# A streaming encoder layer: gate and history loads on GpSimd's queue, gated stores on ScalarE's, new pooling state copied from scratch

## The chip, the cores and the metric

The kernel runs on one core of a Trainium2 chip. The core has a matmul engine (TensorE, PE; its weight loads are listed as PEld), a vector engine (VectorE, DVE), a scalar engine (ScalarE, ACT), GpSimd (POOL) and SyncE (SP, used here to issue DMAs). Each engine works through its own instructions in order; DMAs issued by an engine go through that engine's queue to the shared DMA engines. The metric is the device time of one launch in microseconds (us).

## The reference

One layer for a prompt of 1024 tokens and 8 streams of 16 new tokens each. Cut to what matters here:

```python
xn = rms_norm(x, norm_g)
u, g_pool, c_q, c_kv, k_r, g_mla = jnp.split(xn @ w_in, SPLIT_IDX, axis=-1)
# for each of 4 groups of 256 channels, window w in (2, 4, 8, 16):
#   d = trailing mean over w tokens of u (with 15 tokens of history) - u
#   out = d @ w_pool[group]
pool_out = out * pool_scale * jax.nn.silu(g_pool)
new_pool = jnp.concatenate([pool_hist, u], axis=1)[:, -POOL_HIST:]     # POOL_HIST = 15
...                                                                    # latent attention -> attn
mla_out = attn * jax.nn.silu(g_mla)
h = x + jnp.concatenate([pool_out, mla_out], axis=-1) @ w_out
y = h + sigmoid(rms_norm(h, ple_norm_g) @ w_ple_gate + b_ple_gate) * (p @ w_ple)
```

For the prompt the history is zero; for each of the 8 streams it is the 15 last rows of its state. `new_pool`, one of the outputs, holds the last 15 rows of u: one set for the prompt and eight for the streams, and it is called `npool` in the kernel.

## The kernel before, in words

All activations lie with channels on the 128 partitions and tokens along the free axis. The 1152 tokens (1024 of the prompt, 128 of the streams) are three blocks t = 0, 1, 2 of 384; the third has the prompt's last 256 tokens and the 128 of the streams. Products are taken in three matmuls of a high and a low part (`wh`, `wl`, written by ScalarE and VectorE from the raw weights `wraw`), L77 to L79 or L175 to L177.

The first phase is the input projection. Its output columns are tiles of 128 channels, taken two at a time ("pairs" m), in the order: latents, then for each of the four groups g two tiles gp (the pool branch's gate) and two tiles u (the pool branch's input), then eight tiles gm (the attention's gate). It runs in two chunks of the reduction: the first leaves partial sums in DRAM scratch, the second reads them back (tile `q`, L512, on SyncE's queue), adds, and calls `finish` on each result `o`, which multiplies, takes Silu of gp and gm on ScalarE (L534), and stores to scratch in DRAM (L535, on GpSimd's queue). In the trace, the source or destination `gp`, `gm`, `u` is that scratch; in the order, `gp0`, `gp1`, `gp2` and `u0`, `u1`, `u2` are the scratch of the three token blocks.

While the second chunk goes on to the next pairs, the mixer works on the group that is done. `mixer(m, i)` is called between the parts of a pair and takes two steps from a list for each call. The steps of a group:
- `fetch` loads a block of u back from scratch on SyncE's queue (tile `u`, two buffers): L704 the 384 tokens, L703 the 15 tokens ahead of them; for t = 2 also L707, the streams' history, from the input `state_pool` into tile `us`.
- `weights` loads `w_pool` (L673, SyncE) and splits it into `pwh`, `pwl`.
- `gates` loads two tiles of Silu(gp) (L713, SyncE) into tile `ev`, which has two buffers.
- `tile` forms the windowed means on VectorE (L689, L693, and L727, L728 for the first tokens), giving `d`. For t = 2 it copies the streams' tokens to `us` and stores the new state from the SBUF tiles to the output, on GpSimd's queue: L730 from `u` (128 x 15), L734 from `us` (128 x 8 x 15, runs of 60 bytes).
- `split` makes `dh` (ScalarE, L68) and `dl` (VectorE, L69).
- `mix` multiplies by the group's weights (TensorE, L77 to L79 into `aux`), scales by pool_scale and the gate on VectorE (L751, into the gate's tile `ev`) and stores to scratch `mixp` on GpSimd's queue (L752).

The program is traced through a tile framework: buffers of a name are reused in turn, an instruction waits by semaphore for those that it depends on, and a scheduler sets the order of each engine's instructions by its own costs. So the place of an instruction in its queue isn't the one in the code. `k.later` and `step` only decide in which order things are traced. After the first phase come the latents and keys, the attention, and the output projection with the embedding gate.

Of the kernel before, what the change touches and what calls it, by code (L numbers as in the profile page):

```python
# [16 lines left out]
NB = 8  # L17
NS = 16
NTOK = SEQ + NB * NS
P = 128  # L20
# [3 lines left out]
HIST = 15  # L24
# [106 lines left out]
class Quick:  # L131
# [47 lines left out]
    def pair(self, c0, c1, A, X, W, prior, done, between):  # L179
# [23 lines left out]
        q = prior and prior(c0, 0)  # L203
        self.product(a, x("11"), W[1], True)
        s1 = tile("s1", 2)
        nc.scalar.activation(s1[:], a, AF.Copy)
        d = bank(c1, 1)
# [45 lines left out]
def phase1(k, sc):  # L253
# [4 lines left out]
    tc, nc, io = k.tc, k.nc, k.io  # L258
# [6 lines left out]
    pp = es.enter_context(tc.tile_pool(name="p1m", bufs=1, space=PSUM, reuse_waits="tile"))  # L265
# [12 lines left out]
    src = [io["w_in"][first[n] + i] for n, i in kinds]  # L278
# [10 lines left out]
    def o_tile():  # L289
        return k.t(xp, [P, TB], "o", bufs=3)  # L290
# [48 lines left out]
    def step(n=1):  # L339
        for _ in range(n):  # L340
            if steps:
                steps.pop(0)()


    raw = k.t(wp, [P, 8, P], "wraw", bufs=3)
# [156 lines left out]
    for n in OPS:  # L502
        for j in range(4):
            raw = k.t(ap, [P, TB], f"a{j}")
# [12 lines left out]
    def latent_factor(kind, t, a):  # L517
        yield
        yield from factors(lp, a, 3, KVR if kind == "ckv" else QR, 3)
        nc.sync.dma_start(sc["s_" + kind][t][:], a[:])  # L520

    def finish(i, t, ps, q):
        kind, n = kinds[i] if i < KR else ("kr", 0)
        o = o_tile()
        if q is not None:
            nc.vector.tensor_tensor(o[:], ps, q[:], ALU.add)
            ps = o[:]
        if t == 2:
            nc.vector.tensor_tensor(o[:], ps, R2[:], ALU.mult)
        if kind == "kr":  # L530
            k.later(rope_key(k, lp, aux_bank, o, kc, ks, t, sc))
            return
        if kind in ("gp", "gm"):
            nc.scalar.activation(o[:], o[:], AF.Silu)  # L534
        nc.gpsimd.dma_start(sc[kind][t][:, n, :], o[:])  # L535
        if kind not in ("ckv", "cq"):
            return
        if (kind, t) not in acc:
            acc[kind, t] = [k.t(lp, [P, TB], f"acc{t}"), 2 if kind == "ckv" else 4]
            nc.scalar.activation(acc[kind, t][0][:], o[:], AF.Square)  # L540
        else:
            sq = k.t(lp, [P, TB], "sq")
            nc.scalar.activation(sq[:], o[:], AF.Square)
            nc.vector.tensor_tensor(acc[kind, t][0][:], acc[kind, t][0][:], sq[:], ALU.add)
        acc[kind, t][1] -= 1
        if not acc[kind, t][1]:
            k.later(latent_factor(kind, t, acc[kind, t][0]))
# [8 lines left out]
    def mixer(m, i):  # L556
        k.tick()
        if m < 5:
            return
        if not mix:  # L560
            assert not k.queue
            ls.close()
            mp = es.enter_context(tc.tile_pool(name="p1p", bufs=1, side="right", reuse_waits="tile"))
            inv = k.t(mp, [P, 16], "inv")
            nc.sync.dma_start(inv[:], io["inv_cnt"])
            mix.append(Pool(k, mp, aux_bank, inv, sc, wp))
        pool = mix[0]
        if m in (5, 7, 9, 11) and i == 0:
            g = (m - 5) // 2
            for t in range(NT):  # L570
                if t == 0:
                    pool.fetch(2 * g, 0)
                steps.append(lambda t=t: (pool.fetch(2 * g + 1, t), pool.tile(2 * g, t)))
                steps.append(lambda t=t: pool.tile(2 * g + 1, t))
                if t:
                    steps.append(lambda t=t: pool.mix(g, t - 1))
                else:
                    steps.append(lambda: pool.weights(g))
                steps.append(lambda t=t: (pool.gates(g, t), t < NT - 1 and pool.fetch(2 * g, t + 1), pool.split()))
            steps.append(lambda: pool.mix(g, NT - 1))  # L580
        step(2)

    chunk(1, prior, finish, mixer, range(KR // 2 - 1), KR - 2 * 3)
    last = KR // 2 - 1
    W = qk.sums(src[2 * last:], 1, True)
    qk.pair(2 * last, 2 * last + 1, A, None, W, prior, finish, lambda i: mixer(last, i))
    qk.tail()
    wn = (qk.hl(qk.raw(src[KR - 2 * 3], 1)), 0)
# [38 lines left out]
def rope_key(k, lp, aux_bank, x, kc, ks, t, sc):  # L627

    nc = k.nc
    yield  # L630
    a = aux_bank()
    av = a[:, :TB].rearrange("p (j c) -> p j c", j=3)
    for j in range(3):
        nc.tensor.transpose(av[:, j, :], x[:, j * P:(j + 1) * P], k.ident[:])
    hl = k.t(lp, [P, 3, P], "krhl")
    nc.scalar.activation(hl[:], av, AF.Copy)
    kr = k.t(lp, [P, 3, DR], "kr")
    nc.vector.tensor_tensor(kr[:], hl[:, :, :DR], hl[:, :, DR:], ALU.add)
    tmp = k.t(lp, [P, 3, DR], "krt")
    nc.vector.tensor_tensor(tmp[:], kr[:], kr[:], ALU.mult)  # L640
    v = k.t(lp, [P, 3], "krv")
    r = k.t(lp, [P, 3], "krr")
    nc.vector.tensor_reduce(v[:], tmp[:], AX.X, ALU.add)
    nc.vector.tensor_scalar(v[:], v[:], 1.0 / DR, EPS, ALU.mult, ALU.add)
    k.rsqrt(lp, r[:], v[:], "krs")
    nc.vector.tensor_tensor(kr[:], kr[:], r[:].unsqueeze(2).to_broadcast([P, 3, DR]), ALU.mult)
    o = k.t(lp, [P, 3, 2, DR], "kro")
    sl = slice(3 * t, 3 * t + 3)
    rotate(k, o[:, :, 0, :], kr[:], tmp[:], kc[:, sl, :], ks[:, sl, :], nc.vector)
    nc.vector.tensor_copy(o[:, :, 1, :], o[:, :, 0, :])  # L650
    nc.sync.dma_start(k.io["krope"][:, sl, :], o[:, :, 0, :])
    yield
    yield
    b = aux_bank()
    for j in range(3):
        nc.tensor.transpose(b[:, j * P:(j + 1) * P], o[:, j, :, :].rearrange("p a c -> p (a c)"), k.ident[:])
    e = k.t(lp, [P, TB], "ev")
    nc.scalar.activation(e[:], b[:, :TB], AF.Copy)
    nc.sync.dma_start(sc["krT2"][t][:], e[:])


class Pool:


    def __init__(self, k, pp, aux_bank, inv, sc, wp):
        self.k, self.pp, self.aux, self.inv, self.sc = k, pp, aux_bank, inv, sc
        self.wp, self.hl, self.d = wp, [None, None], [None, None]
        self.u, self.gate, self.us = {}, {}, {}

    def weights(self, g):  # L670
        k, pp = self.k, self.pp
        raw = k.t(self.wp, [P, 8, P], "wraw", bufs=3)[:, :4, :].rearrange("p (a b) c -> p a (b c)", a=2)
        k.nc.sync.dma_start(raw, k.io["w_pool"][g])  # L673
        self.wh = k.t(pp, [P, 2, 256], "pwh", F32R)
        self.wl = k.t(pp, [P, 2, 256], "pwl", F32R)
        k.split(self.wh[:], self.wl[:], raw)
# [19 lines left out]
    def fetch(self, ct, t):  # L696

        k, nc, src = self.k, self.k.nc, self.sc["u"]
        u = self.u[ct, t] = k.t(self.pp, [P, HIST + TB], "u", bufs=2)
        if t == 0:  # L700
            nc.vector.memset(u[:, :HIST], 0.0)
        else:
            nc.sync.dma_start(u[:, :HIST], src[t - 1][:, ct, TB - HIST:])  # L703
        nc.sync.dma_start(u[:, HIST:], src[t][:, ct, :])  # L704
        if t == NT - 1:
            us = self.us[ct] = k.t(self.pp, [P, NB, HIST + NS], "us", bufs=2)
            nc.sync.dma_start(us[:, :, :HIST], self.k.io["state_pool"][ct])  # L707

    def gates(self, g, t):
        k = self.k  # L710
        for n in (2 * g, 2 * g + 1):
            self.gate[n, t] = k.t(self.pp, [P, TB], "ev", bufs=2)
            k.nc.sync.dma_start(self.gate[n, t][:], self.sc["gp"][t][:, n, :])  # L713

    def tile(self, ct, t):
        k, pp, nc, io = self.k, self.pp, self.k.nc, self.k.io
        g, c2 = divmod(ct, 2)
        w = 2 << g
        d = self.d[c2] = k.t(pp, [P, TB], f"d{c2}")
        n = TB if t < NT - 1 else SEQ - TB * (NT - 1)  # L720
        u = self.u.pop((ct, t))
        s = self.window(u[:, :HIST + n], n, d[:, :n], w)
        if t == 0:

            m = w - 1
            x = k.t(pp, [P, 16], "head")
            nc.vector.tensor_tensor(x[:, :m], s[:, HIST:HIST + m], self.inv[:, :m], ALU.mult)  # L727
            nc.vector.tensor_tensor(d[:, :m], x[:, :m], u[:, HIST:HIST + m], ALU.subtract)  # L728
        if t == NT - 1:
            nc.gpsimd.dma_start(io["npool"][ct][:, 0, :], u[:, n:n + HIST])  # L730
            us = self.us.pop(ct)
            nc.vector.tensor_copy(us[:, :, HIST:], u[:, HIST + n:].rearrange("p (b s) -> p b s", b=NB))
            self.window(us[:], NS, d[:, n:].rearrange("p (b s) -> p b s", b=NB), w, (NB,))
            nc.gpsimd.dma_start(io["npool"][ct][:, 1:, :], us[:, :, NS:])  # L734

    def split(self):
        for c, d in enumerate(self.d):
# [944 lines left out]
```

## Time and profile before

| | |
|---|---|
| runs (us) | 2287.53, 2289.75, 2299.92; median 2289.75 |
| the profiled execution | 2292.38 us, its span 2290.6 us |
| TensorE | 2211.1 us busy, 97% of the span |
| VectorE, ScalarE, GpSimd | 1439.5, 1004.0, 410.8 us busy |
| DMA | 339.24 MB, mean 148 GB/s |

A row of the trace's timeline gives start, duration, engine (SPq is SyncE's issuing of DMAs), line, operation, out<-in, shapes and, in brackets, the idle time ahead of the instruction on its engine with what ended it. The line numbers are those of the kernel before. DMA rows give the time from issue to landing. Where a stretch is given as A:B, it is in us from the span's start. The mixer of the four groups lies between about 515 and 800 us.

### The profile page before, as it was taken

To read this page: it belongs to the slowest core of one execution; us is meant where nothing else is said; L and a number is where in the kernel's file an instruction comes from. 1 tells how busy PE (TensorE), PEld (TensorE's weight loads), DVE (VectorE), ACT (ScalarE), POOL (GpSimd) and SP (SyncE) were. 2 spreads that over 40 slices of the span, in tenths; PEclk is the share of its full clock that TensorE was granted. 3 is DMA by queue.
4 is the path that set the end of the run, shared out by engine and by line. 5 is a ranking of instruction groups with operands and counts; after the bars stand their busy time and mean duration, and the time that the engine had idled before them with its cause. 6 is when DMAs were issued, how large, how long until landed. Compare 5 with 4: busy or idle time off the path is not lost.

```text
span 2290.6 us, 36006 instructions
## 1 busy us (share of the span) xinstructions
PE 2211.1 (97%) x12856; PEld 2154.0 (94%) x12856; DVE 1439.5 (63%) x3008; ACT 1004.0 (44%) x2229; POOL 410.8 (18%) x431
## 2 busy tenths in 40 slices
PE   8989999999898989989999899999999999999999
PEld 7989999999898989989998799999999999999998
DVE  6787776686777667768888765555553345344343
ACT  6533335443333467766666644343342233232232
POOL 0000000111222101034453532221002221111110
PEclk9999999999999999999999899999999999999999
DMA  9565336557766666473221754443263333222221
GB/s 303 178 225 169 125 125 213 166 161 192 190 185 179 216 206 179 130 240 99 93 84 53 241 179 152 128 154 122 85 198 112 101 121 110 86 94 96 85 87 64
DMA packets 241012, 339.24 MB, mean 148 GB/s; under 512 B 37729, under 2 KB 185313, under 8 KB 240833
## 3 DMA queue, kind: packets, MB, share of 16 engines
q1 hardware_dynamic: 217568, 290.77, 41.3%
q0 software_dynamic: 10880, 32.41, 4.4%
q10 hardware_dynamic: 12384, 13.77, 1.9%
q8 instruction: 101, 1.65, 0.3%
q14 instruction: 79, 0.64, 0.1%
HBM read 235.74 MB, written 101.12 MB: 147 GB/s over the span
## 4 chain that ended last, share of the span: by engine, by line
PE 66%; DMA 12%; DVE 9%; issue 8%; ACT 3%; POOL 2%; SPq 0%; ACTq 0%; DVEq 0%; POOLq 0%
PE mm L78 8%; PE mm L77 8%; PE mm L79 8%; PE mm L175 5%; PE mm L176 5%; PE mm L177 5%; PE f L77 3%; PE f L79 3%; PE f L78 3%; PE k L79 2%; PE k L78 2%; PE k L77 2%; DMA u<-u 1%; PE t L1215 1%; PE pb L77 1%
## 5 line engine op out<-in xcount | busy, mean ns | idle before, releaser
L68 ACT ACTIVATE wh<-wraw 128x1024 fp32r<-128x1024 f32 (+3 forms) x207 | 150.2, 729 | 146.3 <-PE mm L177 83.8
L69 DVE TENSOR_TENSOR wl<-wraw,wh 128x512 fp32r<-128x512 f32 (+3 forms) x205 | 172.0, 842 | 66.7 <-ACT wh L68 58.8
L1538 DVE TENSOR_TENSOR ev<-mm,R 128x384 f32<-128x384 f32 x48 | 26.7, 557 | 173.9 <-PE mm L79 170.0
L1539 ACT ACTIVATE ev<-ev,gains 128x384 f32<-128x384 f32 x48 | 29.4, 612 | 224.2 <-DVE ev L1538 124.4
L71 ACT ACTIVATE wh<-wraw,gains 128x128 fp32r<-128x128 f32 x256 | 82.1, 391 | 53.0 <-ACT wh L71 31.9
L72 DVE SCALAR_TENSOR_TENSOR wl<-wraw,gains,wh 128x128 fp32r<-128x128 f32 x256 | 88.0, 390 | 18.0 <-ACT wh L71 16.9
L77 PE MATMUL k<-wkh,ch 128*128 128x448 f32 x256 | 96.1, 376 | 3.2 <-ACT ch L68 2.7
L1216 ACT ACTIVATE pth<-t 128x512 fp32r<-128x512 f32 (+2 forms) x96 | 45.5, 485 | 119.7 <-PE t L1215 117.9
L68 ACT ACTIVATE wh<-wt 128x1024 fp32r<-128x1024 f32 x60 | 63.4, 1056 | 74.0 <-PE mm L177 48.5
L78 PE MATMUL k<-wkh,cl 128*128 128x448 f32 x256 | 94.5, 369 | 0.1
L79 PE MATMUL k<-wkl,ch 128*128 128x448 f32 x256 | 94.6, 369 | 0.0
L69 DVE TENSOR_TENSOR wl<-wt,wh 128x1024 fp32r<-128x1024 f32 x60 | 73.3, 1221 | 24.8 <-ACT wh L68 24.6
L79 PE MATMUL mm<-A2l,wh 128*128 128x384 f32 x256 | 86.0, 336 | 0.0
L77 PE MATMUL mm<-A2h,wh 128*128 128x384 f32 x256 | 86.0, 336 | 0.0
L78 PE MATMUL mm<-A2h,wl 128*128 128x384 f32 x256 | 86.0, 336 | 0.0
L77 PE MATMUL mm<-A0h,wh 128*128 128x384 f32 x256 | 85.8, 335 | 0.0
L79 PE MATMUL mm<-A0l,wh 128*128 128x384 f32 x256 | 85.7, 335 | 0.0
L78 PE MATMUL mm<-A1h,wl 128*128 128x384 f32 x256 | 85.7, 335 | 0.0
L78 PE MATMUL mm<-A0h,wl 128*128 128x384 f32 x256 | 85.7, 335 | 0.0
L77 PE MATMUL mm<-A1h,wh 128*128 128x384 f32 x256 | 85.5, 334 | 0.0
L79 PE MATMUL mm<-A1l,wh 128*128 128x384 f32 x256 | 85.5, 334 | 0.0
L1510 POOL TENSOR_TENSOR R<-R,sq 128x384 f32<-128x384 f32 x45 | 46.0, 1023 | 210.3 <-ACT sq L1509 210.3
(809 smaller groups left out, 7867.2 us busy)
## 6 DMA issues: line engine op xcount, KB each, us to landing
wraw<-w_in SPq DMA_DIRECT2D x89, 512.0 KB, 4.4
part<-o SPq DMA_DIRECT2D x93, 192.0 KB, 2.5
q<-part SPq DMA_DIRECT2D x93, 192.0 KB, 3.1
wraw<-w_out SPq DMA_DIRECT2D x64, 256.0 KB, 3.3
wraw<-w_ple_gate SPq DMA_DIRECT2D x64, 256.0 KB, 3.2
ple<-ev POOLq DMA_DIRECT2D x48, 192.0 KB, 2.9
fev<-xT SPq DMA_DIRECT2D x48, 192.0 KB, 2.5
hp<-fev SPq DMA_DIRECT2D x48, 192.0 KB, 2.1
```

The lines of the kernel that those rows point to most:

```text
L68: nc.scalar.activation(hi, src, AF.Copy)
L69: eng.tensor_tensor(lo, src, hi, ALU.subtract)
L71: nc.scalar.activation(hi, src, AF.Copy, scale=scale)
L72: eng.scalar_tensor_tensor(lo, src, scale, hi, ALU.mult, ALU.subtract)
L77: mm(out, sh, mh, start=start, stop=False)
L78: mm(out, sl, mh, start=False, stop=False)
L79: self.last = mm(out, sh, ml, start=False, stop=stop)
L175: mm(ps, sh, xh[:], start=start and j == 0, stop=False, **kw)
L176: mm(ps, sl, xh[:], start=False, stop=False, **kw)
L177: self.k.last = mm(ps, sh, xl[:], start=False, stop=j == n - 1, **kw)
L1216: nc.scalar.activation(pth[:, :n, qq], tp[:, :n, :], AF.Copy)
L1510: nc.gpsimd.tensor_tensor(acc[t][:], acc[t][:], sq[:], ALU.add)
```

## The change

Three things are moved, and one is done in another way:
- The stores of gp and gm (48) are issued by ScalarE instead of GpSimd. The stores of u and of the latents stay on GpSimd.
- The loads of the gates (24) and of the streams' history (8) are issued by GpSimd instead of SyncE.
- The new pooling state is no longer stored from the SBUF tiles but copied from the scratch of u (block 2) to the output, DRAM to DRAM, in the same two pieces for each channel tile (16 DMAs), on GpSimd's queue as before.
- The load of w_pool is traced earlier in a group: behind the first fetch.

```diff
@@ finish
+        store = nc.gpsimd
         if kind in ("gp", "gm"):
             nc.scalar.activation(o[:], o[:], AF.Silu)
-        nc.gpsimd.dma_start(sc[kind][t][:, n, :], o[:])
+            store = nc.scalar
+        store.dma_start(sc[kind][t][:, n, :], o[:])
@@ mixer
                 if t == 0:
                     pool.fetch(2 * g, 0)
+                    pool.raw_weights(g)
@@ Pool
+    def raw_weights(self, g):
+        self.raw = self.k.t(self.wp, [P, 8, P], "wraw", bufs=3)[:, :4, :].rearrange("p (a b) c -> p a (b c)", a=2)
+        self.k.nc.sync.dma_start(self.raw, self.k.io["w_pool"][g])
+
     def weights(self, g):
-        k, pp = self.k, self.pp
-        raw = k.t(self.wp, [P, 8, P], "wraw", bufs=3)[:, :4, :].rearrange("p (a b) c -> p a (b c)", a=2)
-        k.nc.sync.dma_start(raw, k.io["w_pool"][g])
+        k, pp, raw = self.k, self.pp, self.raw
@@ fetch
-            nc.sync.dma_start(us[:, :, :HIST], self.k.io["state_pool"][ct])
+            nc.gpsimd.dma_start(us[:, :, :HIST], self.k.io["state_pool"][ct])
@@ gates
-            k.nc.sync.dma_start(self.gate[n, t][:], self.sc["gp"][t][:, n, :])
+            k.nc.gpsimd.dma_start(self.gate[n, t][:], self.sc["gp"][t][:, n, :])
@@ tile
         if t == NT - 1:
-            nc.gpsimd.dma_start(io["npool"][ct][:, 0, :], u[:, n:n + HIST])
             us = self.us.pop(ct)
             ...
-            nc.gpsimd.dma_start(io["npool"][ct][:, 1:, :], us[:, :, NS:])
+            src = self.sc["u"][t][:, ct, :]
+            nc.gpsimd.dma_start(io["npool"][ct][:, 0, :], src[:, n - HIST:n])
+            nc.gpsimd.dma_start(io["npool"][ct][:, 1:, :], src[:, n:].rearrange("p (b s) -> p b s", b=NB)[:, :, NS - HIST:])
```

In the changed kernel the stores of `finish` are L537, the histories L708 (u) and L712 (us), the block fetch L709, w_pool L675, the gates L718, the new state L740 and L741, `mixp` L759.

The scheduler's order around the start of the second group, on GpSimd. Names carry a buffer number; `o` is a finished result, `ev` a gate tile. Before:

```order
L752 DMA mixp2_15_74<-ev_1150_5802 128x384
L752 DMA mixp2_15_74<-ev_1151_5804 128x384
L535 DMA u2_27_86<-o_1162_5877 128x384
L535 DMA u2_27_86<-o_1163_5904 128x384
L535 DMA u1_26_85<-o_1184_5986 128x384
L535 DMA u0_25_84<-o_1185_6001 128x384
L535 DMA gp0_7_66<-o_1198_6044 128x384
```

The same place now:

```order
L759 DMA mixp2_15_74<-ev_1150_5802 128x384
L759 DMA mixp2_15_74<-ev_1151_5804 128x384
L537 DMA u2_27_86<-o_1162_5877 128x384
L718 DMA ev_1202_6066<-gp0_7_66 128x384
L718 DMA ev_1203_6068<-gp0_7_66 128x384
L740 DMA npool<-u2_27_86 128x15
L741 DMA npool<-u2_27_86 128x8x15
L537 DMA u2_27_86<-o_1163_5904 128x384
L740 DMA npool<-u2_27_86 128x15
L741 DMA npool<-u2_27_86 128x8x15
L537 DMA u1_26_85<-o_1184_5986 128x384
L537 DMA u0_25_84<-o_1185_6001 128x384
```

The new state's pieces, which stood further back, between gp stores of the next tiles, now stand directly behind the store of u's block 2 that they read, two pairs of them ahead of the stores of blocks 1 and 0, and two gates have come in between; the gp store is gone from this queue.

SyncE's queue at the same place, before. `u_1187` in it is the tile for block 0 of the group's odd channel tile, `wraw` the raw weights, `part1x` the first chunk's partial sums:

```order
L673 DMA wraw_1199_6060<-w_pool 128x512
L704 DMA u_1204_6070<-u1_26_85 128x384
L512 DMA q_1250_6259<-part11_29_88 128x384
L512 DMA q_1267_6342<-part12_30_89 128x384
L143 DMA wraw_1233_6212<-w_in 128x1024
L704 DMA u_1187_6007<-u0_25_84 128x384
L143 DMA wraw_1234_6214<-w_in 128x1024
```

The same place now (the odd tile's block 0 is `u_1188` here):

```order
L675 DMA wraw_1187_6007<-w_pool 128x512
L512 DMA q_1250_6259<-part11_29_88 128x384
L512 DMA q_1267_6342<-part12_30_89 128x384
L709 DMA u_1204_6070<-u1_26_85 128x384
L143 DMA wraw_1233_6212<-w_in 128x1024
L709 DMA u_1188_6009<-u0_25_84 128x384
L143 DMA wraw_1234_6214<-w_in 128x1024
```

Two loads of partial sums have moved ahead of the fetch of u's block 1; the fetch of the odd tile's block 0 stays ahead of the load of the next weights.

## The prediction

> **What bounds the kernel now.** I read the page's head, then the stage of the mixer by windows, then the matmuls with an idle stretch ahead of them, then what those wait for.
>
> ```profile
> span 2290.6 us, 36006 instructions
> 515.00:800.00 285.00, 267.10 (x1484) 264.70 (x1483) 198.11 (x379) 99.02 (x164) 57.58 (x102) 0.97 0.69 191
> 640.00:655.00 15.00, 15.00 (x88) 15.00 (x87) 8.93 (x13) 6.38 (x10) 2.16 (x4) 1.00 0.65 206
> 620.00:630.00 10.00, 6.26 (x27) 5.94 (x26) 7.72 (x15) 2.30 (x4) 1.62 (x3) 0.83 1.01 273
> 685.00:695.00 10.00, 7.38 (x41) 6.74 (x40) 5.79 (x13) 0.91 (x2) 1.08 (x2) 1.00 0.81 237
> 740.00:755.00 15.00, 8.56 (x39) 8.25 (x38) 8.68 (x20) 2.48 (x5) 1.62 (x3) 0.77 0.80 191
> ```
>
> The window rows give length, busy time and count of PE, PEld, DVE, ACT and POOL, the granted clock, the DMA share and GB/s. The diff touches 515 to 800 us, apart from the stores, which begin with the second chunk. There TensorE is busy 267.10 of 285.00 us: it is the bound, and only its idle stretches can be won or added. An undisturbed stretch makes 88 matmuls in 15 us, 5.87 per us. That is the scale for the three disturbed windows, since it counts slow clock as well as idle time.
>
> ```profile
> 564.73 0.41 PE L77 MATMUL aux<-dh,pwh 128*128 128x384 f32 x1 [0.71 <-DVE ev L751]
> 601.78 0.44 PE L77 MATMUL aux<-dh,pwh 128*128 128x384 f32 x1 [2.50 <-ACT dh L68]
> 625.43 0.44 PE L77 MATMUL aux<-dh,pwh 128*128 128x384 f32 x1 [3.74 <-ACT dh L68]
> 690.24 0.45 PE L77 MATMUL aux<-dh,pwh 128*128 128x384 f32 x1 [1.48 <-ACT dh L68]
> 748.73 0.69 PE L175 MATMUL mm<-22_0h,wh 128*128 128x384 f32 x1 [6.43 <-DVE u L221]
> 621.09 1.23 DVE L69 TENSOR_TENSOR wl<-wraw,wh 128x1024 fp32r<-128x1024 f32 x1 [4.98 <-DMA npool<-u]
> 687.09 0.56 DVE L526 TENSOR_TENSOR o<-mm,u 128x384 f32<-128x384 f32 x1 [3.81 <-DMA gp<-o]
> 747.59 0.62 DVE L751 SCALAR_TENSOR_TENSOR ev<-aux,gains,ev 128x384 f32<-128x384 f32 x1 [5.79 <-DMA ev<-gp]
> ```
>
> In brackets stand the idle time ahead of the instruction and what ended it. Three of the stretches have one DVE instruction behind them: at 621.09 it waits for the history output to leave the u tile, at 687.09 for a gp store that stands behind it in GpSimd's queue, at 747.59 for a gate that SyncE issued late.
>
> **What it wins.** From the windows, lost time is (88/15 × length − count) / 5.87: (58.7 − 27)/5.87 = 5.4 us at 620, (58.7 − 41)/5.87 = 3.0 at 685, (88 − 39)/5.87 = 8.4 at 740. With the 0.71 at 564.73, also a late gate, 17.5 us. The outputs no longer hold the u and us tiles, the gp and gm stores go on ScalarE's queue, the gates leave SyncE's: I count all 17.5 as gained, the upper bound; the lower is nothing, if the same lines find another late DMA. The 2.50 at 601.78 stays: there u of an odd tile is late, which the change doesn't hasten.
>
> **What it costs: the outputs' new place.** On GpSimd the output of a channel tile, 128x15 and then 128x8x15, now follows the store of u's last token block, and must first wait until that store has landed. GpSimd's queue is in order. Behind it stand the same block of the odd channel tile, that tile's own output pair with the same wait, and then blocks 1 and 0 of u for the next group, which SyncE fetches back.
>
> ```profile
> L730 POOL DMA_DIRECT2D npool<-u x8: 538/541/559, 546.6 to 734.6; - x8
> L734 POOL DMA_DIRECT2D npool<-us x8: 901/901/904, 547.5 to 735.1; - x8
> DMA to landing us min/median/max: 2.1/3.4/12.0
> DMA to landing us min/median/max: 6.7/8.3/11.9
> gp<-o POOLq DMA_DIRECT2D x1, 192.0 KB, 10.1
> mixp<-ev POOLq DMA_DIRECT2D x1, 192.0 KB, 8.1
> gm<-o POOLq DMA_DIRECT2D x1, 192.0 KB, 8.2
> gp<-o POOLq DMA_DIRECT2D x1, 192.0 KB, 11.9
> 610.00:620.00 10.00, 10.00 (x60) 10.00 (x59) 5.54 (x15) 3.48 (x5) 2.95 (x5) 1.00 0.92 117
> ```
>
> The issues take 0.54 and 0.90 us (min/median/max in ns). The first landing row is that of the stores L535, median 3.4; the second that of L734, median 8.3. The next four are the stores that GpSimd issued right behind an L734, at 548.9, 609.4, 731.9 and 675.2: they land in 10.1, 8.1, 8.2 and 11.9 us, since the 1024 runs of 60 bytes are ahead of them. At 610 the engines are busy 0.92 of the time for 117 GB/s, where 640 to 655 has 0.65 for 206. No row shows such runs copied from scratch. By the nearest rows they land between 3.4 (as a store of whole rows) and 11.9; I take the mean of the four, L = 9.6, because source and destination both have the same short runs.
>
> The Trainium skill, DMA: Bandwidth & Descriptors, section Anatomy of one DMA, puts a GpSimd-issued DMA at about 2.0 us plus bytes over 436e3; for 61,440 bytes that is an estimate of 2.14 us. The trace's 8.3 for L734 disagrees. The same page, section Specifications, asks for at least 512 bytes per transfer for the full rate; L734's runs of 60 bytes beside the 3.4 of the whole rows agree with that. By the formula there would be no delay below, and the kernel would be faster (the first rival).
>
> With X the issue of the even tile's store, the block 0 of the odd tile lands at X + 3.4 (first store) + 1.44 (two issues) + L (odd store behind the runs) + 1.44 + 0.54 (issue of block 1) + L = X + 6.8 + 2L, X + 26.0 at L = 9.6. Until then SyncE stands at that tile's fetch, with the loads of partial sums (q) and of w_in behind it in its queue.
>
> ```profile
> 517.23 0.54 POOL L535 DMA_DIRECT2D u<-o  x1 [2.01 <-DVE o L529]
> 578.75 0.54 POOL L535 DMA_DIRECT2D u<-o  x1 [0.39 <-DVE o L529]
> 588.24 0.54 POOL L535 DMA_DIRECT2D u<-o  x1 [1.06 <-DVE o L526]
> 635.89 0.54 POOL L535 DMA_DIRECT2D u<-o  x1
> 690.33 0.54 POOL L535 DMA_DIRECT2D u<-o  x1 [1.85 <-DVE o L529]
> 535.92 0.32 SPq L704 DMA_DIRECT2D u<-u  x1
> 592.76 0.42 SPq L704 DMA_DIRECT2D u<-u  x1
> 650.93 0.42 SPq L704 DMA_DIRECT2D u<-u  x1
> 710.50 0.38 SPq L704 DMA_DIRECT2D u<-u  x1
> 541.40 0.53 ACT L68 ACTIVATE dh<-d 128x384 fp32r<-128x384 f32 x1 [0.46 <-DVE d L728]
> 544.72 0.34 PE L77 MATMUL aux<-dh,pwh 128*128 128x384 f32 x1
> 660.05 0.53 ACT L68 ACTIVATE dh<-d 128x384 fp32r<-128x384 f32 x1 [0.90 <-DVE d L728]
> 662.12 0.34 PE L77 MATMUL aux<-dh,pwh 128*128 128x384 f32 x1
> ```
>
> The even tiles' stores X at the four groups' starts are at 517.23, 578.75, 635.89 and 690.33; SyncE's fetches of the odd block 0 at 535.92, 592.76, 650.93 and 710.50.
> - First group: 517.23 + 26.0 = 543.2, 7.3 later; TensorE used dh 544.72 − (541.40 + 0.53) = 2.8 after it was ready, so 4.5 remain.
> - Second: 604.7, 12.0 later, on top of the 2.50 already waited there: 12.0.
> - Third: 661.9, 11.0 later; slack 662.12 − (660.05 + 0.53) = 1.5; and the mixer's matmuls now stand 9 further back in TensorE's order, 9/5.87 = 1.5. Remain 8.0.
> - Fourth: four small issues (two mixp stores, a gate, a us history; 3 × 0.54 + 0.90 = 2.5) come between: 718.8, 8.3 later, less 10/5.87 = 1.7 by the order. Remain 6.6.
>
> Together 31.1 us. With L at 8.1 and 11.9 each loses or gains twice the difference, 8 × 1.5 = 12 less or 8 × 2.3 = 18 more: 19 to 49.5. A stall also lowers the granted clock: the windows at 620 and 740 lost 5.4 and 8.4 where their stalls last 3.74 and 6.43, so 1.7 and 2.0 more each. Two of the four are stalls where there was none as long (third, fourth): 3.6 more.
>
> **Costed at nothing.**
>
> ```profile
> L788 ACTq DMA_DIRECT2D wraw<-w_ple x48: 334/334/1362, 810.5 to 1278.4; - x48
> SPq L713 <- DMA mixp<-ev: 26.0, 15, 9.1
> ```
>
> The 48 stores of gp and gm on ScalarE's queue: 48 × 0.334 = 16 us of issue; ScalarE is busy 99.02 of 285.00 us there, and each issue comes right after the Silu it stores, on the same engine. If that cover were gone (loads of mm and dh right behind them), 16 us at most. SyncE loses 24 gate issues with their waits (26.0 us in 15) and 8 histories; it has other waits in the same places. GpSimd takes them: 24 × 0.54 + 8 × 0.90 = 20 us beside 57.58 busy of 285; a gate that waits there for the tile's former mixp store holds back what stands behind it, the second rival. w_pool's load is traced earlier but stands beside the same neighbours on SyncE: nothing either way.
>
> **The sum.** −17.5 + 31.1 + 3.6 = +17.2. The profiled execution took 2292.38 (its span 2290.6), so 2309.6 like for like; the median of the runs, 2289.75, lies 2.6 lower: 2307. With the unknown price at its ends, +5 to +36; the loss of the gains adds up to 17.5 more.
>
> **Rivals.**
> - **The copies are quick (other side).** If runs copied from scratch land like the stores at 3.4, block 0 of the odd tile could land at X + 13.6; in the second group that is 592.3, when SyncE fetched at 592.76 anyway. No delay, and −17.5: 2272. It decides where the 31.1 shrink by 17.2, that is at L = 9.6 − 17.2/8 = 7.5 us. For it: 128x15 before is only 128 runs, and the copy leaves SBUF's tiles alone; against it: the 8.1 to 11.9 behind L734.
> - **GpSimd's queue becomes the wait for the gates too.** Gates of the third token block now wait for mixp stores with us histories in the same queue; DVE's ev would stand as at 747.59, at 8.4 each. Three of them: 2307 + 25 = 2332. For it: mixp stores are themselves behind the copies; against: the first block's gates stand ahead of the copies.
> - **It cancels out.** TensorE's order, with the mixer's matmuls 9 to 10 later, absorbs another 1.5 in the first and second group, and L is about 8: gain and cost meet, 2290.
>
> **How the numbers follow.** Forecast 0.48, quick copies 0.25, gates 0.10, cancelling 0.17. About 0.5% (11.4 us) is what a measurement can tell from no change. The forecast's own range, L from 8.1 to 11.9, is 2295 to 2325 (12 less, 18 more); of its 0.48, 0.06 lies within 11.4 us of no change and 0.42 above. Faster 0.25 (the quick copies), same 0.23 (0.17 + 0.06), slower 0.52 (0.42 + 0.10). The range takes in most of the quick case and the gates: 2268 to 2332.
>
> **What the changed profile would show.** Right: GpSimd waits about 3 us ahead of each output pair; stores of u behind them land in over 8 us; SyncE's odd fetches of block 0 come 7 to 12 us later; the aux matmuls L77 wait 4 to 14 us for dh at the four group starts; the stalls at 621, 687 and 747 are gone. Wrong: if the copies land in under 6 us, or the scheduler's order lets SyncE pass other loads ahead, the starts show no stall and the time falls. If the window from 800 us on, where the diff has nothing but held-back gm stores, differs by more than a few us, the whole reasoning misses something.

## The result, and the profile after

Over 20 runs of each the changed kernel took 2298.68 us (median; 2292.10 to 2303.05), the kernel before 2291.34 (2286.31 to 2299.92): ratio 1.0031, 95% interval 1.0021 to 1.0040. It is 7.1 us slower (0.31%), where 17 us slower was forecast.

The profiled execution took 2303.05 us, the longest of the 20, so its trace overstates the loss: its span is 10.7 us longer than that of before. The page's head, the mixer's stage by windows, and the windows around the four groups' starts (same columns as before):

```profile
span 2301.3 us, 35933 instructions
515.00:800.00 285.00, 264.69 (x1469) 262.66 (x1468) 195.78 (x377) 100.19 (x162) 57.03 (x95) 0.96 0.67 187
530.00:560.00 30.00, 27.23 (x144) 26.20 (x143) 21.35 (x45) 10.89 (x18) 3.08 (x6) 0.94 0.62 170
590.00:620.00 30.00, 20.59 (x107) 20.27 (x106) 14.52 (x26) 8.06 (x14) 2.52 (x4) 0.83 0.63 147
665.00:680.00 15.00, 9.91 (x47) 9.59 (x46) 11.77 (x24) 4.71 (x9) 0.00 (x0) 0.77 0.59 185
725.00:740.00 15.00, 11.96 (x60) 11.63 (x60) 12.69 (x27) 4.17 (x9) 0.00 (x0) 0.89 0.43 135
```

In 285 us 1469 matmuls were made instead of 1484: up to 800 us the stage lost 15/5.87 = 2.6 us. But the stalls are in other places. The matmuls with an idle stretch of more than 0.6 us ahead of them are now these five, and no other up to the stage's end:

```profile
541.47 0.44 PE L77 MATMUL aux<-dh,pwh 128*128 128x384 f32 x1 [1.47 <-ACT pwh L68]
550.27 0.44 PE L77 MATMUL aux<-dh,pwh 128*128 128x384 f32 x1 [1.02 <-ACT dh L68]
613.33 0.69 PE L77 MATMUL aux<-dh,pwh 128*128 128x384 f32 x1 [9.41 <-ACT dh L68]
674.89 0.69 PE L77 MATMUL aux<-dh,pwh 128*128 128x384 f32 x1 [5.09 <-ACT dh L68]
733.83 0.69 PE L77 MATMUL aux<-dh,pwh 128*128 128x384 f32 x1 [3.04 <-ACT dh L68]
```

The three stalls of before with a DVE instruction behind them (625, 690, 749) are gone, and each group's start has one (the first has two). The next rows are what GpSimd does at the second group's start (timeline), what it waits for in the stage (waits: total, times, longest), and how long the copies and the stores behind them take to land (source view of L741; DMA issues at 587.8 and 597.0):

```profile
586.35 0.54 POOL L740 DMA_DIRECT2D npool<-u  x1 [2.72 <-DMA u<-o]
586.88 0.90 POOL L741 DMA_DIRECT2D npool<-u  x1
587.77 0.57 POOL L537 DMA_DIRECT2D u<-o  x1
POOL npool L740 <- DMA u<-o: 30.9, 8, 7.1
DMA to landing us min/median/max: 6.0/7.3/8.7
u<-o POOLq DMA_DIRECT2D x1, 192.0 KB, 7.0
u<-o POOLq DMA_DIRECT2D x2, 192.0 KB, 6.9
```

GpSimd waits 30.9 us in eight times for the landing of u's block 2, and the stores of u that stand behind the copies land in 7 us instead of 3.4. So far it is the forecast's mechanism.

Behind the mixer there is a second difference. In each block the first row is the first product of the latents, the second the last transposition of `mx` in the streams' attention, and the last row a product of the output projection. Before, then after:

```profile
810.60 0.61 PE L77 MATMUL pb<-wkh,ckvh 128*128 128x512 f32 x1 [3.51 <-ACT wqh L68]
1262.89 0.30 PE L1370 MATMUL aux<-ident,mx 128*128 128x128 f32 x1 [1.07 <-DVE mx L1368]
1683.33 0.34 PE L77 MATMUL mm<-M1h,wh 128*128 128x384 f32 x1
```

```profile
815.87 0.77 PE L77 MATMUL pb<-wkh,ckvh 128*128 128x512 f32 x1 [6.08 <-ACT wqh L68]
1265.90 0.30 PE L1377 MATMUL aux<-ident,mx 128*128 128x128 f32 x1 [1.05 <-DVE mx L1375]
1334.79 0.66 PE L77 MATMUL f<-M2h,wh 128*128 128x384 f32 x1 [3.52 <-DVE s L1202]
1692.20 0.34 PE L77 MATMUL mm<-M1h,wh 128*128 128x384 f32 x1
```

The latents start 5.3 us later, with 6.08 us of idle ahead of their first product instead of 3.51. From the transposition to the product of the output projection it was 1683.33 − 1262.89 = 420.4 us, and is 1692.20 − 1265.90 = 426.3, with an idle stretch of 3.52 us in it that before didn't have. Some of that is won back between the two, so that the part from the first product of the latents to the end of the span grew from 1480.0 to 1485.4 us: half of the span's 10.7.

The diff touches nothing there. What differs is the order: of TensorE's 8557 matmuls from the first product of the latents on, 1722 stand at another place than before. Why the scheduler comes to this order was not looked into.

### The profile page after: what moved, and what is told of

Read it like the earlier page. It is cut to its first block, busy times and chain, and to the rows that moved or that the text cites. A ratio compares the mean times of both kernels' runs of the same rounds, so it can differ in the third digit from the quotient of the medians.

```text
span 2301.3 us, 35933 instructions
## 1 busy us (share of the span) xinstructions
PE 2214.1 (96%) x12856; PEld 2158.4 (94%) x12856; DVE 1442.1 (63%) x3008; ACT 1002.9 (44%) x2229; POOL 407.5 (18%) x415
## 4 chain that ended last, share of the span: by engine, by line
PE 71%; DMA 12%; DVE 7%; issue 5%; ACT 3%; POOL 2%; SPq 1%; ACTq 0%; POOLq 0%; DVEq 0%
PE mm L77 8%; PE mm L79 8%; PE mm L78 8%; PE mm L175 6%; PE mm L177 6%; PE mm L176 6%; PE f L77 3%; PE f L79 3%; PE f L78 3%; DMA u<-o 2%; PE k L78 2%; PE k L77 2%; PE k L79 2%; PE pb L79 1%; PE pb L77 1%
```

## The experiments

Besides these two, fifteen runs were made, two of them repeats. The ratios are those to the kernel before, run on the same chip in the same batch (A to D); the interval is 95%. A and B ran on one chip, C and D on one other each, so rows of one batch compare best.

| kernel | batch | ratio, interval | new state, 60-byte runs | gm stores | last interval (us) |
|---|---|---|---|---|---|
| before | – | 1 | from tiles | GpSimd | 420.4 |
| changed (20 runs) | – | 1.0031, 1.0021 to 1.0040 | copies, early | ScalarE | 426.3 |
| changed, again | D | 1.0034, 1.0022 to 1.0045 | copies, early | ScalarE | 429.4 |
| copies behind block 0 | A | 1.0062, 1.0043 to 1.0081 | copies, behind block 0 | ScalarE | 427.8 |
| copies behind mixp | C | 1.0010, 0.9998 to 1.0022 | copies, behind mixp | ScalarE | 428.1 |
| output from tiles | A | 1.0022, 1.0010 to 1.0034 | from tiles | ScalarE | 425.8 |
| gm on GpSimd | A | 1.0007, 0.9992 to 1.0022 | copies, early | GpSimd | 420.3 |
| gm on GpSimd, again | D | 1.0009, 1.0000 to 1.0019 | copies, early | GpSimd | 419.5 |
| both edits | A | 1.0047, 1.0030 to 1.0063 | copies, behind block 0 | GpSimd | 419.5 |
| copies alone | B | 1.0036, 1.0023 to 1.0049 | copies, early | GpSimd | 418.2 |
| gp and gm stores alone | B | 1.0044, 1.0031 to 1.0058 | from tiles | ScalarE | 424.8 |
| gm stores alone | C | 1.0011, 1.0001 to 1.0021 | from tiles | ScalarE | 425.9 |
| gates and histories alone | B | 1.0018, 1.0004 to 1.0033 | from tiles | GpSimd | 421.5 |
| changed, 128x15 copies only | B | 0.9957, 0.9943 to 0.9971 | 128 of 1152 each | ScalarE | 427.8 |
| changed, packed | D | 0.9942, 0.9928 to 0.9955 | none | ScalarE | 423.1 |
| changed, packed, gm on GpSimd | C | 0.9933, 0.9918 to 0.9948 | none | GpSimd | 422.9 |
| before, packed | C | 0.9907, 0.9893 to 0.9921 | none | GpSimd | 424.1 |

The last column is the interval shown above, from the transposition to the product of the output projection, in each kernel's profiled execution.

**Copies behind block 0.** An order edge keeps the copies behind the last store of u of their group:

```diff
+            with k.tc.issue_after(k.u_stored[g]):     # the store of u, odd tile, t = 0
                 nc.gpsimd.dma_start(io["npool"][ct][:, 0, :], ...)
                 nc.gpsimd.dma_start(io["npool"][ct][:, 1:, :], ...)
```

> The changed kernel with one order edge more: the 16 copies of the new state stay on GpSimd's queue, but stand behind the store of u's block 0 of the odd channel tile instead of ahead of it. All else is the same, the order of the later phases too. Theory (the copies' place delays u's stores, and so SyncE's fetches): the four stalls at the groups' starts, worth about 20 us, vanish, the gains of the change stay; about 2279 us, ratio to the kernel before 0.994 to 0.996. Rival 1 (the copies' short runs cost DMA time wherever they stand): no gain, 2296 to 2300, ratio 1.002 to 1.004, the stalls only move. Rival 2 (the stalls are waits for something else at the groups' starts, gates or w_pool): unchanged stalls, ratio 1.003.

It takes 1.0062, where the theory had 0.994 to 0.996. The theory fell here, and the first rival, that the runs cost DMA time wherever they stand, had named too little. The cleanest pair is in the same batch: gm on GpSimd (1.0007) and both edits (1.0047) differ in the copies' place alone, and the later place loses 0.40%, 9 us. At the second group's start (GpSimd without the two 128x15 copies, SyncE, then three DMAs with their time to landing, the DMA engines by a window, and TensorE):

```profile
591.00 0.54 POOL L537 DMA_DIRECT2D u<-o  x1 [1.05 <-DVE o L526]
592.06 0.90 POOL L745 DMA_DIRECT2D npool<-u  x1
593.47 0.89 POOL L745 DMA_DIRECT2D npool<-u  x1
595.02 0.33 SPq L143 DMA_DIRECT2D wraw<-w_in  x1
595.40 0.43 SPq L712 DMA_DIRECT2D u<-u  x1
wraw<-w_in SPq DMA_DIRECT2D x1, 512.0 KB, 11.9
u<-u SPq DMA_DIRECT2D x1, 192.0 KB, 12.0
gp<-o ACTq DMA_DIRECT2D x1, 192.0 KB, 10.8
595.00:610.00 15.00, 11.14 (x64) 10.82 (x63) 5.88 (x11) 2.65 (x3) 0.00 (x0) 1.00 0.84 137
611.23 0.69 PE L77 MATMUL aux<-dh,pwh 128*128 128x384 f32 x1 [5.09 <-ACT dh L68]
```

GpSimd's store of block 0 is now ahead of the copies, and SyncE issues the odd tile's fetch 9 us earlier (595.40, against 604.35 in the changed kernel). But that fetch lands after 12.0 us, the w_in load ahead of it after 11.9, and a gp store on ScalarE's queue after 10.8. The copies are under way on another queue, and the DMA engines are busy 0.84 of the time for 137 GB/s, where the undisturbed stretch of before has 0.65 for 206. So a copy costs more than a place in GpSimd's queue: transfers of the other queues are slow while it drains.

The Trainium skill, DMA: Bandwidth & Descriptors, section Queues, rings and completion order, says that each DMA engine takes turns between the queues and drains a whole packet from one before it goes to the next. The 11.9 and 12.0 us of SyncE's loads beside GpSimd's copies agree with that; no run here shows the turns themselves.

**gm on GpSimd**, then run again beside the changed kernel on one chip:

```diff
-        if kind in ("gp", "gm"):
-            nc.scalar.activation(o[:], o[:], AF.Silu)
-            store = nc.scalar
+        if kind in ("gp", "gm"):
+            nc.scalar.activation(o[:], o[:], AF.Silu)
+        if kind == "gp":
+            store = nc.scalar
```

> The changed kernel with the 24 gm stores back on GpSimd's queue (gp stays on ScalarE's). The scheduler then orders everything behind the mixer as in the kernel before. Theory (of the 7.3 us that the change cost, some 3 are in the mixer and some 4 behind it, from the order that the gm stores on ScalarE's queue bring about): about 2294 us, ratio 1.001 to 1.002, the start of the latents at the offset of the mixer's end, 3 us. Rival (all is the mixer's, the later phases differ by chance of one execution): 2298, ratio 1.003.

> The changed kernel as it is. Theory (part of its cost is in the mixer, part behind it): ratio 1.002 to 1.004; in its profile the mixer's end within 6 us of before's, and again a loss of 5 to 8 us between 1260 and 1500 us. Rival (the loss behind the mixer was chance): no loss there.

> The changed kernel with the gm stores on GpSimd, on the same chip as the changed kernel. Theory: 4 to 6 us less than the changed kernel, ratio 1.000 to 1.002. Rival (the earlier difference came from the chip): the same time as the changed kernel, ratio 1.002 to 1.004.

On one chip 1.0034 (changed) stands against 1.0009: 0.25%, 5.7 us. With the gm stores back on GpSimd TensorE's 8557 matmuls behind the mixer come in the order of before again, every one, and the last interval is that of before, without the idle stretch. Changed kernel, second execution, then the same with gm on GpSimd:

```profile
1255.76 0.30 PE L1377 MATMUL aux<-ident,mx 128*128 128x128 f32 x1 [1.06 <-DVE mx L1375]
1326.34 0.66 PE L77 MATMUL f<-M2h,wh 128*128 128x384 f32 x1 [3.52 <-DVE s L1202]
1685.13 0.34 PE L77 MATMUL mm<-M1h,wh 128*128 128x384 f32 x1
```

```profile
1256.98 0.30 PE L1378 MATMUL aux<-ident,mx 128*128 128x128 f32 x1 [1.06 <-DVE mx L1376]
1676.45 0.34 PE L77 MATMUL mm<-M1h,wh 128*128 128x384 f32 x1
```

The table's last column says the same over the kernels that aren't packed: with gm on ScalarE 424.8 to 429.4 in eight executions, without it 418.2 to 421.5 in six. TensorE's order behind the mixer is one and the same in the eight, and that of before in the six. The column overstates the loss, since the part ahead of the transposition is some 3 us shorter in the eight. From the first product of the latents to the end they take 1483.2 to 1489.3 us (mean 1485.4), the six 1479.2 to 1482.8 (mean 1481.1): 4.3 us more. The idle stretch just ahead of that product is 4.3 to 6.5 us in the eight and 2.9 to 3.7 in the six: 2.3 more. Together that is 6.6, near the 5.7 of the pair.

The three packed kernels are between, at 422.9 to 424.1. Two of them have an order of their own; the one with gm on GpSimd has that of before and still 422.9, so some us of this interval hang on something else. Between packed (0.9942) and packed with gm on GpSimd (0.9933) no loss by the gm stores can be told.

The second execution of the changed kernel has shorter stalls at the groups' starts than the first, 10.6 us in three instead of 20.0 in five:

```profile
552.69 0.44 PE L77 MATMUL aux<-dh,pwh 128*128 128x384 f32 x1 [2.49 <-ACT dh L68]
612.74 0.69 PE L77 MATMUL aux<-dh,pwh 128*128 128x384 f32 x1 [4.95 <-ACT dh L68]
673.28 0.59 PE L77 MATMUL aux<-dh,pwh 128*128 128x384 f32 x1 [3.18 <-ACT dh L68]
```

So the stalls in the mixer of one execution carry some 9 us of chance, or of the chip, and the split between the mixer and what follows rests on the times of all runs.

**Both edits, and the parts alone.** The first has the copies behind block 0 and gm on GpSimd; the others take one part of the change into the kernel before, or the copies out of the changed kernel.

> Both edits together: copies behind the store of u's block 0 of the odd tile, gm stores on GpSimd's queue. By both theories the mixer gains 17 us and nothing is lost behind it: about 2275 us, ratio 0.992 to 0.994. If only the first holds, 2279 (0.995); if only the second, 2294 (1.001); if neither, 2298 (1.003).

> The changed kernel with the new state stored from the SBUF tiles as in the kernel before (the copies undone, the rest kept). Theory: the four stalls at the groups' starts (about 20 us) vanish, and of the old stalls only the one in which the output holds the u tile (5.4 us) comes back: 2298.7 - 20 + 5.4, about 2284 us, ratio 0.996 to 0.998. Rival (the stalls come from gates and histories in GpSimd's queue): they stay, 2296 to 2304, ratio 1.002 to 1.006.

> The kernel before with the copies from scratch alone (stores of gp and gm on GpSimd, gates and histories on SyncE as before). Theory: the four stalls at the groups' starts appear (about 20 us), the stall at 621 us goes (5.4), the two others of before stay: +15, about 2306 us, ratio 1.005 to 1.008, and the later phases in their old order add nothing. Rival (the stalls need the gates in GpSimd's queue too): 2286 to 2291, ratio 0.997 to 1.000.

> The kernel before with the stores of gp and gm on ScalarE's queue alone. Theory: the stall at 690 us (3.0) goes; the later phases take the order of the changed kernel and lose some 4 us: 2292 us, ratio 0.999 to 1.002, with the loss behind the mixer's end. Rival (that order costs nothing): 2288, ratio 0.998 to 0.999.

> The kernel before with the gates and histories on GpSimd's queue alone. Theory: the stall at 748 us (8.4) and the small one at 565 us (0.7) go, the later phases keep their order: 2282 us, ratio 0.995 to 0.997. Rival (behind the outputs and gp stores in GpSimd's queue the gates come as late as before): 2291 or more, ratio 1.000 to 1.004.

> The kernel before with the 24 gm stores alone on ScalarE's queue. Theory (the order of the later phases that this brings about costs 5 to 7 us between 1260 and 1500 us): the mixer's end at most 3 us earlier than before, then a loss of 5 to 7; ratio 1.001 to 1.003, with an idle stretch of over 3 us of TensorE ahead of an output-projection product near 1330 us. Rival (the loss came with the gates or the copies): ratio 0.998 to 1.000, no such stretch.

Both edits: 1.0047, above all four values that were expected: the loss of the late copies without the loss behind the mixer (1.0062 with it). Output from tiles: 1.0022, where 0.996 to 0.998 was expected. The stalls came back elsewhere, one of them at the second group's gates and one at the third's start:

```profile
626.46 0.44 PE L77 MATMUL aux<-dh,pwh 128*128 128x384 f32 x1 [2.12 <-DVE ev L756]
662.75 0.69 PE L77 MATMUL aux<-dh,pwh 128*128 128x384 f32 x1 [2.89 <-ACT dh L68]
```

Copies alone: 1.0036, 8 us and not 15; the stalls at the starts are there (5.58 and 5.46), and the one of the late gate, 6.43 at 748.73 before, is 0.97 at 747.60 though its gate is still SyncE's:

```profile
606.46 0.69 PE L77 MATMUL aux<-dh,pwh 128*128 128x384 f32 x1 [5.58 <-ACT dh L68]
667.68 0.69 PE L77 MATMUL aux<-dh,pwh 128*128 128x384 f32 x1 [5.46 <-ACT dh L68]
```

Gates and histories alone: 1.0018 where 0.995 to 0.997 was expected; in its place the stall waits for VectorE's ev, with the gates behind the outputs in GpSimd's queue, and 3.88 at 748 is left of the 6.43. gp and gm stores alone: 1.0044, above the expected range; why more than gm alone (1.0011, as expected) was not found. In both, the idle stretch of over 3.5 us ahead of the output projection's product is there, at 1324.59 and 1322.63:

```profile
624.39 0.66 PE L77 MATMUL aux<-dh,pwh 128*128 128x384 f32 x1 [4.74 <-DVE ev L751]
748.33 0.44 PE L175 MATMUL mm<-S_0h,wh 128*128 128x384 f32 x1 [3.88 <-DVE o L526]
1322.63 0.66 PE L77 MATMUL f<-M2h,wh 128*128 128x384 f32 x1 [3.52 <-DVE s L1195]
```

(The first two are of gates alone, the last of gm alone.) Whatever is moved, as long as the short runs stay, stalls of together 10 to 22 us stay in the mixer and change places.

**Copies behind mixp.** The same order edge, to the second mixp store of the group's first block.

> The changed kernel with the copies of the new state moved, by an order edge, behind the two mixp stores of the group's first token block, some 25 us later than in the changed kernel, where SyncE's fetches of the odd tile's block 0 are long done. Behind them in GpSimd's queue stand the gates of the second block. Theory (the copies' short runs occupy the DMA engines for some 7 us each pair, and what that costs depends on what is due then): no stall at the groups' starts, the gates behind land in over 8 us and may open a shorter stall 10 to 20 us later; 2284 to 2292 on the scale of 2291 for before, ratio 0.997 to 1.001. Rival (their DMA time is lost wherever they stand): ratio 1.003 to 1.006.

1.0010. No stall over 1.2 us at the starts; the largest is the one that was expected, behind late gates, in the third group:

```profile
681.37 0.66 PE L77 MATMUL aux<-dh,pwh 128*128 128x384 f32 x1 [4.30 <-DVE ev L759]
DMA to landing us min/median/max: 6.2/9.0/12.9
wraw<-w_in SPq DMA_DIRECT2D x1, 512.0 KB, 14.5
```

The second row is the landing of its 128x8x15 copies, the third SyncE's w_in load issued some 3 us behind the third group's, at 669.5. In each of the four groups the w_in load behind the copies took 13.2 to 14.5 us. Each against before on its own chip, this place is some 5 us better than that of the changed kernel (1.0034) and 12 better than the one behind block 0 (1.0062): what the runs cost depends on which DMA is due while they drain, but no place tried makes them free.

**Fewer short runs, or none.** First the changed kernel without its 128x8x15 copies; it leaves the streams' part of the new state unwritten. Then the state packed by VectorE into the first 135 columns of the u tile, which is dead by then, and stored in one DMA; this in the changed kernel, in the same with gm on GpSimd, and in the kernel before.

```diff
+            nc.vector.tensor_copy(u[:, :HIST], u[:, n:n + HIST])
+            nc.vector.tensor_copy(u[:, HIST:9 * HIST].rearrange("p (b s) -> p b s", b=NB), us[:, :, NS:])
+            nc.gpsimd.dma_start(io["npool"][ct].rearrange("p b s -> p (b s)"), u[:, :9 * HIST])
-            nc.gpsimd.dma_start(io["npool"][ct][:, 0, :], ...)
-            nc.gpsimd.dma_start(io["npool"][ct][:, 1:, :], ...)
```

> The changed kernel with the 128x15 copies in their place, but without the eight copies of 128x8x15 (the streams' part of the new state is not written). Theory (the 1024 short runs hold back the stores behind them): stores behind the copies land in 3 to 4 us instead of 6 to 8.5, the odd fetch comes some 7 us earlier, the stalls at the groups' starts fall by half or more: 2284 to 2291 us, ratio 0.997 to 1.000. Rival (the waits for the landing of u's block 2 ahead of each copy alone make the delay): stalls as in the changed kernel, ratio 1.002 to 1.004.

> The changed kernel with the new state packed in the u tile and stored in runs of 540 bytes; gates, histories and the stores of gp and gm as in the changed kernel. Theory (the 60-byte runs cost the changed kernel about 20 us in the mixer; the order behind it still costs 5): 2268 to 2278 on before's 2287, ratio 0.993 to 0.996, no stall of TensorE over 2 us at the groups' starts. Rival (place and waits cost, not the runs): 1.000 or more.

> The changed kernel with the new state packed by VectorE in the u tile and stored in one DMA of 128 runs of 540 bytes, and with the gm stores on GpSimd. Theory (the short runs cost the changed kernel some 17 us in the mixer, gm on ScalarE some 5 behind it): 17 us less than before's 2291 in the mixer, 2272 to 2278, ratio 0.992 to 0.995. Rival (the u tile is held by the store again, as at 621 us before): 2280 to 2286, ratio 0.995 to 0.998.

> The kernel before, with the new state put together by VectorE (two copies) in the first 135 columns of its own u tile and stored in one DMA of 128 runs of 540 bytes instead of 128 of 60 and 1024 of 60. Nothing else is moved. Theory (the runs of 60 bytes hold back the stores behind them and keep the u tile): the stalls at 625 and 690 us shorten, the late gate at 749 stays; 2282 to 2287 of 2291, ratio 0.996 to 0.998. Rival (the runs were hidden in the kernel before): 2291, ratio 0.999 to 1.002.

0.9957, 0.9942, 0.9933 and 0.9907. The first leaves the 128x15 copies and their waits in place, and is 17 us below the changed kernel by the ratios (1.0034): the waits for the landing of block 2 are not the cost, the 128x8x15 copies are. On one chip the changed kernel is at 1.0034 and the packed one at 0.9942: 0.92%, 21 us, with 128 runs of 540 bytes a tile for 1152 of 60. That shows that it is the runs and not the bytes, though this pair moves the store as well, 19 to 31 us back to where before had it; before and before with packing have it in about the same place and differ by as much. The packed store has 7.5 KB more than the 128x8x15 copy and lands in half its time. Windows of the stage in packed, and in before with packing, then the landing times of their stores:

```profile
515.00:785.00 270.00, 264.06 (x1509) 262.23 (x1508) 203.45 (x404) 103.54 (x170) 49.36 (x86) 1.00 0.67 208
515.00:780.00 265.00, 264.39 (x1514) 263.56 (x1512) 203.37 (x404) 103.50 (x169) 51.20 (x95) 1.00 0.68 212
DMA to landing us min/median/max: 2.1/3.6/4.4
DMA to landing us min/median/max: 2.7/3.9/4.8
```

In before with packing TensorE is idle 0.6 us of 265, where before had 17.9 of 285. Nearly all that this part of the kernel stood still for went with the short runs of its outputs, the late gates and the held u tile among it, though gates and gp stores are issued by the same engines as before. Only 0.996 to 0.998 was expected, with the late gate left. It beats both kernels: 2265.18 us, 21 us less than before on its chip. In the same batch the packed kernel with the change's other parts and gm on GpSimd took 2270.60: once the short runs are gone, those parts lose some 5 us.

The Trainium skill, DMA: Bandwidth & Descriptors, section Rules for kernel authors, says to coalesce many small transfers into one large, and section Specifications wants 512 bytes or more per transfer for the full rate. The 540-byte runs, landing in 3.6 us beside the 60-byte runs in 7.3, agree with both.

## Why the prediction was right and wrong

- **The gains, 17.5 us.** Right as to the places: the stalls at 625, 690 and 749 and the small one at 565 are absent in both executions of the changed kernel. That they were each the work of one late instruction was too narrow: before with packing has none of them either, though its gates stay on SyncE and its gp stores on GpSimd.
- **The mechanism of the cost.** Right as far as it went: GpSimd waits for the landing of u's block 2, the stores behind land late, and SyncE's fetches and dh are late at all four starts. What was missing is that the same runs hold up transfers of other queues: with the copies behind block 0 the order that the prediction blamed is gone, and more is lost.
- **The size of L** is the term that was mis-sized in the mixer: 9.6 us taken, 8.1 to 11.9 as bounds, measured 6.1 to 8.5 over the eight stores behind copies, mean 7.0, below the lower bound. By the prediction's formula that takes 8 × 2.6 = 21 off the 31.1, and the sum of the costs would be 31.1 − 21 + 3.6 = 14. The reason given for a large L was wrong as well: only the source has runs of 60 bytes. In the output the eight sets of one partition lie in a row, 480 bytes. And copying from scratch landed about like storing from the tile: 7.3 us here, 8.3 before, 7.3 again in "output from tiles".
- **The fetches.** The odd tiles' block 0 was fetched at 543.09, 604.35, 664.77 and 723.13, which is 25.7, 23.2, 22.3 and 25.2 us behind the even tiles' stores X (517.39, 581.19, 642.45, 697.95); forecast were 26.0 and, in the fourth group, 28.5. So part of what L had too much was made up by waits that the formula left out. At the second start the first landing took 5.2 us, from 581.19 to GpSimd's 586.35, and not 3.4, since two gates are in between; in the first group a store waited 1.56 us for its result. With the shift of X itself taken off, the fetches are 28.5 us late in all, where 38.6 was forecast.
- **The stalls at the starts.** Against the forecast 34.7 (31.1 + 3.6) on top of what stood there, this execution lost, by matmul counts, (176 − 144)/5.87 = 5.5, (176 − 107)/5.87 = 11.8, (88 − 47)/5.87 = 7.0 and (88 − 60)/5.87 = 4.8, together 29.1; before lost 3.7 and 3.4 at two of these places:

```profile
590.00:605.00 15.00, 12.50 (x66) 12.17 (x65) 11.03 (x21) 5.31 (x9) 1.62 (x3) 0.92 0.64 211
710.00:725.00 15.00, 13.12 (x68) 12.79 (x67) 13.00 (x26) 5.17 (x10) 2.16 (x4) 0.90 0.49 157
```

  So 22.0 us are new, in the worse of two executions. The 28.5 us by which the fetches are late, less the slack of 7.5 that the prediction counted (2.8 + 3.0 + 1.7), give 21: its path from fetch to stall holds, what it had too large is the delay that goes in. Gains of 17.5 and costs of 22.0 make +4.5 in this execution's mixer, and the latents start 5.3 later.
- **Nothing behind 800 us.** Wrong, and the step that failed most plainly: the prediction put no term there, and had itself named a difference from 800 us on as the sign that its reasoning misses something. The 48 stores moved to ScalarE were costed at nothing by their issue time. That time was as forecast, 0.33 us each in the median. But their effect is on the order: by the pair on one chip 5.7 us of the 7.1 come from the gm stores, with the idle stretches ahead of the latents and of the output projection. How the order costs these us is not shown. Put into the kernel before alone, the gm stores cost 0.11%, 2.5 us, so the 5.7 holds beside the other parts of the change.
- **The sum.** With gm on GpSimd the change is worth 1.0009 (1.0000 to 1.0019): mixer gain and mixer cost meet. That was the rival "it cancels out" at 0.17, though not by its reason (L about 8 and absorption by TensorE's order). The 17 us forecast had too much in the mixer and nothing behind it; that the kernel came out slower, as forecast, is largely luck, since most of the loss comes from the term that was left out.
- **The rivals.** "The copies are quick": L came to 7.0, below the 7.5 at which the formula gives a gain, and yet the kernel didn't become faster, with gm on GpSimd neither (1.0009). The formula left out the waits named above and the other queues. "GpSimd's queue becomes the wait for the gates" fell for the changed kernel: no stall behind ev is among its five. It did show in gates alone and in copies behind mixp. The Trainium skill's formula (DMA: Bandwidth & Descriptors, section Anatomy of one DMA), by which the estimate for such a transfer was 2.14 us, is more than three times under the 7.3 measured.

## What to carry to other kernels

Price a DMA by its runs as well as its bytes, and charge it to every queue: two outputs of 1024 runs of 60 bytes made loads of other queues land in 12 us and more, and moving such a DMA between sources or places mostly chose who waits. When several stalls with different names lie in one stage, look for what drains on the DMA engines at those moments before curing each by itself; here two copies on VectorE for each tile cured all of them. Where a scheduler sets the order, a moved instruction has a second cost in whatever is traced after it; compare the order there, and test it by an edit that brings the old order back.

## What the runs showed of the hardware

- Loads of SyncE's queue issued 1.5 to 2 us behind the second of two 128x8x15 copies on GpSimd's landed in 11.9 and 12.0 us, and in copies behind mixp such w_in loads took 13.2 to 14.5; w_in loads took 4.4 in the median of the kernel before.
- An output of 128 runs of 540 bytes instead of 1024 of 60, with an eighth more bytes, landed in 3.6 us for 7.3 in the changed kernel, and in 3.9 for 8.3 in the kernel before (medians). The copies of 128 runs of 60 bytes landed in 2.3 (median, changed kernel with 128x15 copies only).
- The number of short runs alone doesn't set the price. The eight loads of the streams' histories are 128x8x15 too, with the short runs in the tile: the packets under 512 bytes fall from 37729 to 29537, by 8 × 1024, when they leave SyncE's queue (gates and histories alone). They stayed in all kernels, landed in 5.7 us in before, and in 4.2 in the packed ones, where TensorE hardly waits. For GpSimd's outputs the 1024 runs are those of the program: the profile doesn't count them as packets, and packing takes away only 257 under 512 bytes (37729 to 37472). What makes such outputs dearer than such loads was not tested.
- Two executions of one program showed 20.0 and 10.6 us of idle TensorE in the mixer, while the idle stretch behind the mixer was 3.52 us in both.
